# A three-block transformer stack on one core: late transposes behind the next products, and a gated-attention recurrence by 128 tokens

## The chip, the cores and the metric

The kernel runs on one core of one Trainium2 chip. The metric is the device time of one execution in microseconds (us), the median of several runs. TensorE (PE) does the matrix products, VectorE (DVE), ScalarE (ACT) and GpSimd (POOL) the elementwise work, SyncE (SP) issues most transfers. A matrix product reads its stationary operand by a weight load (PEld) of its own and writes to PSUM, which has eight banks here: two named mm, three a, three t.

## The reference

A sequence of 512 tokens of width 1024 (float32) goes through a first block with three branches side by side (gated linear attention, sparse attention over the best 128 keys, cross attention to 256 memory tokens), and then two blocks A and B, each with a mixer, an output projection and an FFN of 2816. Every sublayer has a norm before and after it:

```python
x = x + rmsnorm(merged @ w_o, g_post)          # first block
for l in range(2):
    h = rmsnorm(x, g_mix_pre[l])
    mix = concat([main(h), memory_attention(h)]) @ w_out[l]
    x = x + rmsnorm(mix, g_mix_post[l])
    x = x + rmsnorm(swiglu(rmsnorm(x, g_ffn_pre[l]), w_ffn_in[l], w_ffn_out[l]), g_ffn_post[l])
```

The gated attention (4 heads, keys of 128, values of 256) works in chunks of 64 tokens. With b the running sum of the log gates in a chunk:

```python
q_d = q * exp(b); k_d = k * exp(-b); k_t = k * exp(b_last - b); decay = exp(b_last)
o = tril(q_d @ k_d.T) @ v + q_d @ state       # per chunk and head
state = decay * state + k_t.T @ v
```

## The kernel before

**Products.** Every large product is made of float32 halves: `mm3` (lines 372 to 375) issues high x high, high x low and low x high, so one unit of a 1024-deep weight is 24 matmuls. `unit_T` (404) multiplies one weight block of 128 columns by all 512 tokens (512 columns a matmul), `units_half` (414) takes several weight blocks and does tokens 0 to 255 of all of them before tokens 256 to 511 (256 columns a matmul), `units_N` (427) gives tokens as rows. The plain float32 products of the recurrence and the transposes through the identity are not split; such a product leaves two records in the trace, a transpose one.

**Weights.** Weights come in one packed array, in the order of use. `load_more` (297) issues the transfers on SP into 47 general slots of [128, 1024] (`get`, `put`: the slot that has been free longest is taken first); some weights are scaled on GpSimd as they land (line 310). `do_piece` (334) splits them: ScalarE makes the high half (336), VectorE, or GpSimd where `ctl["lo"]` says so, the low half (337). `ctl["ahead"]` and `ctl["stage"]` say how many weights are split and loaded ahead, and a split begins only while four slots are free (`keep`).

**Order.** The kernel is one unrolled program. Side work (attention blocks) is written as generators that `pump` steps between units. The framework then orders the instructions of each engine itself: by its own estimate of when an instruction's inputs are ready, and among the ready ones by program order. So the order on an engine can differ from that of the program.

**Sublayer ends.** `close_sublayer` (1133) does an output projection for four blocks of 128 tokens. For each block: 48 products into a pair of banks, then `to_T` (492) of the block before (eight transposes through a bank of kind t, ScalarE's high half, VectorE's low half), then `residual` (1100: square sums on ScalarE, the gain product z in 1107, the reciprocal root, x in 1113) and `prenorm` (1121: square sums, reciprocal root, hn in 1128 or 1130). After the fourth block its `to_T` follows at once. `wout` (1301) calls it three times: for `wo` ahead of `mem_kv` (1175, memory keys and values of A), for `awo` and `bwo` ahead of the FFN (1238), which opens with `units_half` over g0, u0, g1, u1 and g2. The FFN's own end (1280 to 1296) has the same loop with banks t t, t a, a a, mm mm for the four blocks; after A's FFN come `mem_kv` of B and the keys `kvk0`, `kvk1` by `units_half` (1619).

**The reciprocal root** (443) is a bit-trick start and two refinements on VectorE, for one value per partition (n = 1) eight instructions: 450, 455, 462, 463, 455, 465, 466 behind the sums of 1091 and 1094.

```python
V.scalar_tensor_tensor(t, y_, v, y_, op0=OP.mult, op1=OP.mult)            # 455
V.scalar_tensor_tensor(t, t, -10.0 / 3.0, t, op0=OP.add, op1=OP.mult)     # 462
V.scalar_tensor_tensor(y, t, 5.0, g, op0=OP.add, op1=OP.mult)             # 463
```

**The recurrence.** `gq` units (954) write qd, `gk` units (971) kd and the decayed keys, which `s_kt` transposes to ktt. `s_gla` (990) is pumped between the units of `dz` and of branch d. For each block of 128 tokens: scores of all 128 x 128 pairs (1017), kept by `copy_predicated` where both tokens are in the same chunk and causal (1019); scores times values (1024); the product of the first chunk's queries with the state into rows 0 to 63 (1027); the state's update from the first chunk's 64 rows, `delta(2t)` (1003 to 1011); then the second chunk's queries with the new state into rows 64 to 127 (1033), `delta(2t + 1)`, and the head norm. The sparse attention `s_dsa` (866) reads queries dq and writes oD (913) in four slots each.

Of the kernel before, what the change touches and what calls it, by code (L numbers as in the profile page):

```python
# [20 lines left out]
D = 1024  # L21
# [137 lines left out]
def make_consts():  # L159
    cols = []  # L160
    pos = 0

    def add(name, arr):
        nonlocal pos
        a = np.zeros((128, arr.shape[1]), np.float32)
        a[:arr.shape[0]] = arr
        _C[name] = (pos, arr.shape[1])
        pos += arr.shape[1]
        cols.append(a)

# [4 lines left out]
    add("bd", ((r[:, None] <= r[None, :]) & (r[:, None] // 64 == r[None, :] // 64)).astype(np.float32))  # L175
# [29 lines left out]
def model_kernel(ctx: ExitStack, tc: tile.TileContext, A, out):  # L205
# [237 lines left out]
    def rsqrt(ss, n, scale, name):  # L443
# [8 lines left out]

        def vyy(y_):
            if n == 1:
                V.scalar_tensor_tensor(t, y_, v, y_, op0=OP.mult, op1=OP.mult)  # L455
            else:
                V.tensor_tensor(t, y_, y_, op=OP.mult)
                V.tensor_tensor(t, t, v, op=OP.mult)

# [5 lines left out]
        V.tensor_scalar(t, t, -0.5 * 0.375 ** 3, 1.5 * 0.375, op0=OP.mult, op1=OP.add)  # L465
# [26 lines left out]
    def to_T(hn, act, tt, keep=False):  # L492

        for j in range(2):
            pt = ps_t([128, 4, 128])
# [368 lines left out]
    oD = [get([128, 2, 512], F32, "oD") for _ in range(4)]  # L864

    def s_dsa():
# [51 lines left out]
        put(*wsel[0], dkT, dvh, dvl, *dq, *toep)  # L918
# [28 lines left out]

    bl = T["b"]
    qd = [get([128, 2, 512], F32, "qd") for _ in range(2)]
    kd = [get([128, 2, 512], F32, "kd") for _ in range(2)]  # L950
    ktt = [get([128, 2, 512], F32, "kt") for _ in range(2)]
    gv = [get([128, 1024], F32, "gv") for _ in range(4)]
    decay = p_c.tile([128, 4, 8], F32, name="decay")
    for h in range(4):
# [4 lines left out]
        V.scalar_tensor_tensor(qd[h // 2][:, h % 2], o, 128 ** -0.5, e, op0=OP.mult, op1=OP.mult)  # L959
        V.tensor_copy(decay[:, h], e[:, 63:512:64])  # L960
        pump()
# [9 lines left out]
    for h in range(4):  # L971
# [4 lines left out]
        V.tensor_tensor(kd[h // 2][:, h % 2], o, e, op=OP.mult)  # L976
# [4 lines left out]
        V.tensor_tensor(flat(e), o, flat(e), op=OP.mult)  # L981
# [8 lines left out]
    def s_gla():  # L990
        att = [get([128, 2, 4, 128], F32, "att")]
        POOL.memset(att[0], 0.0)
        Sb = [get([128, 4, 256], F32, "S") for _ in range(2)]
        bd = C("bd").bitcast(U32)

        def delta(c):
            t, r0 = c // 2, 64 * (c % 2)
            ds = []
            for hp in range(2):
                pa = ps_a([128, 2, 256])  # L1000
                for j in range(2):
                    h = 2 * hp + j
                    PE.matmul(pa[:, j], ktt[t // 2][r0:r0 + 64, t % 2, 128 * h:128 * h + 128],  # L1003
                              gv[t][r0:r0 + 64, 256 * h:256 * h + 256], start=True, stop=True)
                for j in range(2):
                    h = 2 * hp + j
                    if c == 0:
                        V.tensor_copy(Sb[1][:, h], pa[:, j])
                    else:
                        V.scalar_tensor_tensor(Sb[(c + 1) % 2][:, h], Sb[c % 2][:, h], decay[:, h, c:c + 1],  # L1010
                                               pa[:, j], op0=OP.mult, op1=OP.add)

        for t in range(4):
            tk = slice(128 * t, 128 * t + 128)
            pa = ps_a([128, 4, 128])
            for h in range(4):
                PE.matmul(pa[:, h], kd[h // 2][:, h % 2, tk], qd[h // 2][:, h % 2, tk], start=True, stop=True)
            am = att[0][:, t % 2]
            V.copy_predicated(am, bd[:, None, :].to_broadcast([128, 4, 128]), pa)
            yield  # L1020
            po = [ps_t([128, 2, 256]) for _ in range(2)]
            for h in range(4):
                oo = po[h // 2][:, h % 2]
                PE.matmul(oo, am[:, h], gv[t][:, 256 * h:256 * h + 256], start=(h % 2 == 0),
                          stop=False, skip_group_check=True)
                if t:
                    PE.matmul(oo[0:64], qd[h // 2][:, h % 2, 128 * t:128 * t + 64], Sb[0][:, h],
                              start=False, stop=False, skip_group_check=True)
            delta(2 * t)
            yield  # L1030
            for h in range(4):
                oo = po[h // 2][:, h % 2]
                PE.matmul(oo[64:128], qd[h // 2][:, h % 2, 128 * t + 64:128 * t + 128], Sb[1][:, h],
                          start=False, stop=True, skip_group_check=True)
            if t < 3:
                delta(2 * t + 1)
# [11 lines left out]
        put(*att, *Sb, *qd, *kd, *ktt)  # L1048
# [39 lines left out]
    def sums(s2, n):  # L1088
# [44 lines left out]
    def close_sublayer(key, act, gpost, g, a):  # L1133
# [4 lines left out]
        prev = None  # L1138
        for t in range(5):
            if t < 4:  # L1140
                cols = HALVES if t < 3 else LAST
                y = [(ps_a if t % 2 else ps_mm)() for _ in cols]
                for n, sl in enumerate(cols):
                    for k in range(8):
                        mm3(y[n][:, :sl.stop - sl.start], act.hi(k)[:, 128 * t:128 * t + 128], act.lo(k)[:, 128 * t:128 * t + 128],
                            ws[k].hi[:, 0, sl], ws[k].lo[:, 0, sl], k == 0, k == 7)
                tick(2)
                if t == 3:
                    drop(*ws)
                    act.drop()  # L1150
                    ctl["ahead"], ctl["stage"] = 2, 3
            if prev is not None:
                to_T(prev, a, t - 1)
            if t < 4:
                sx = residual(y, t, gpost, cols)
                prev = prenorm(t, sx, g)
            pump()
        ctl["lo"] = None

# [15 lines left out]
    def mem_kv(a, p):  # L1175
# [13 lines left out]
        units_N(f"{p}mv", a, 2, lambda t, o: ACT.activation(v[:, t], o, AF.Copy), ps_a)  # L1189
# [48 lines left out]
    def ffn(p, l, hT, more, side={}):  # L1238
# [4 lines left out]
        first = units_half([f"{p}g0", f"{p}u0", f"{p}g1", f"{p}u1", f"{p}g2"], hT)  # L1243
# [14 lines left out]
        banks = [[ps_t(), ps_t()], [ps_t(), ps_a()], [ps_a(), ps_a()], [ps_mm(), ps_mm()]]  # L1258
# [20 lines left out]
        prev = None  # L1279
        for t in range(5):  # L1280
            if t < 4:
                for n in range(2):
                    for k in range(NFF - NR, NFF):
                        step(k, ws[k - NFF + NR], banks[t][n], t, HALVES[n])
                tick(2)
                if t == 3:
                    drop(*ws)
                    for j in range((NFF - NR) // 2, NFF // 2):
                        act.drop_group(j)
                    ctl["ahead"], ctl["stage"] = 2, 3  # L1290
            if prev is not None:
                to_T(prev, nxt, t - 1)
            if t < 4:
                sx = residual(banks[t], t, gpost, more=more)
                if more:
                    prev = prenorm(t, sx, None)
        gpost.drop()
        ctl["lo"] = None
        return nxt

    def wout(key, act, gpost, gnext):
        gp, g, a = Gain(*gpost), Gain(*gnext), Act(8, "hT")
        close_sublayer(key, act, gp, g, a)
        gp.drop()
        g.drop()
        return a

    memA = mem_prep(0)
    hA = wout("wo", mg, ("g_post",), ("g_mix_pre_2", 0))
    kvm = mem_kv(memA, "a")  # L1310
# [168 lines left out]
    hF = wout("awo", mix, ("g_mix_post_2", 0), ("g_ffn_pre_2", 0))  # L1479
# [30 lines left out]
    hB = ffn("a", 0, hF, True, sides_a)  # L1510
    cosT, sinT = T["rot"]
    memB = T["mem"]
    kvB = mem_kv(memB, "b")
# [123 lines left out]
    hF = wout("bwo", mix, ("g_mix_post_2", 1), ("g_ffn_pre_2", 1))  # L1637
    ffn("b", 1, hF, False)
# [39 lines left out]
```

## Time and profile before

| | |
|---|---|
| median of 3 runs | 2064.12 us (2061.5 to 2064.39) |
| the profiled execution | 2061.36 us, of which the span of its instructions is 2059.6 |
| busy in the span: TensorE | 2000.4 us (97%) |
| VectorE, ScalarE, GpSimd | 1098.4, 807.3, 258.7 us |
| mean granted clock of TensorE | 0.988 |

The profile lists, for a stretch, how long each engine was busy, and for groups of instructions their count, busy time and mean. PEclk is TensorE's granted clock as a share of the full one; it has two levels, 0.50 (1.2 GHz) and 1.00 (2.4 GHz), and values between are means. A matmul's end is modelled and laps over the start of the next.

### The profile page before, as it was taken

What the parts mean: (1) busy time and instruction counts of PE and PEld (TensorE: products, weight loads), DVE (VectorE), ACT (ScalarE), POOL (GpSimd) and SP (SyncE); (2) the same over time, 40 slices, a digit from 0 to 9 for tenths busy, and PEclk for the clock granted to TensorE, in tenths of its full rate; (3) what the DMA queues carried; (4) which work ended last, traced back from release to release, by engine and by line L of the source; (5) the groups of instructions that cost most, each with busy time, mean ns of one, the idle gap of its engine ahead of it and who ended that gap; (6) DMA issues with size and microseconds to landing.
All of it is one profiled execution on the core that took longest, in us unless ns stands there. A gap on an engine that the chain in (4) does not pass through costs nothing.

```text
span 2059.6 us, 26847 instructions
## 1 busy us (share of the span) xinstructions
PE 2000.4 (97%) x10234; PEld 1679.4 (82%) x10234; DVE 1098.4 (53%) x2463; ACT 807.3 (39%) x1787; POOL 258.7 (13%) x214
## 2 busy tenths in 40 slices
PE   7999999999999999999998999999989989999998
PEld 6888878889777888898887888888787778888886
DVE  8744996354654342763677443342668873332423
ACT  5533553244423241444544342232336843322311
POOL 7201100000111111100022111102130021111000
PEclk9999999999999999999999999999999999999999
DMA  6321232122222343232124122144121232322421
GB/s 261 120 72 52 64 113 84 60 82 74 80 72 75 99 144 102 82 126 92 53 81 154 57 93 92 62 154 143 32 82 42 83 126 69 102 72 72 143 73 41
DMA packets 54528, 189.57 MB, mean 92 GB/s; under 512 B 6648, under 2 KB 8832, under 8 KB 54400
## 3 DMA queue, kind: packets, MB, share of 16 engines
q1 hardware_dynamic: 52640, 185.36, 27.5%
q0 software_dynamic: 464, 1.44, 0.3%
q8 instruction: 80, 1.31, 0.3%
q10 hardware_dynamic: 1296, 1.07, 0.2%
q14 instruction: 48, 0.39, 0.1%
HBM read 185.73 MB, written 2.11 MB: 91 GB/s over the span
## 4 chain that ended last, share of the span: by engine, by line
PE 88%; DVE 8%; ACT 2%; issue 1%; DMA 1%; SPq 0%; DVEq 0%; ACTq 0%
PE mm L373 21%; PE mm L375 21%; PE mm L374 21%; PE pa L373 4%; PE pa L375 4%; PE pa L374 4%; PE pt L374 1%; PE pt L375 1%; PE pt L373 1%; PE pt L497 1%; DVE rst L455 1%; PE pa L529 1%; PE pa L1003 1%; PE pa L880 1%; PE pt L1435 1%
## 5 line engine op out<-in xcount | busy, mean ns | idle before, releaser
L509 POOL TENSOR_TENSOR ffal<-t,ffah 128x512 fp32r<-128x512 f32 x44 | 61.3, 1393 | 420.8 <-ACT ffah L508 420.8
L1251 DVE SCALAR_TENSOR_TENSOR t<-t,mm 128x512 f32<-128x512 f32 x42 | 28.8, 685 | 82.5 <-PE mm L375 82.5
L374 PE MATMUL mm<-hTl,h_au 128*128 128x512 f32 (+1 forms) x176 | 66.9, 380 | 0.0
L373 PE MATMUL mm<-hTh,h_bu 128*128 128x512 f32 (+1 forms) x176 | 66.9, 380 | 0.0
L375 PE MATMUL mm<-hTh,l_au 128*128 128x512 f32 (+1 forms) x176 | 66.9, 380 | 0.0
L374 PE MATMUL mm<-hTl,h_bu 128*128 128x512 f32 (+1 forms) x176 | 66.9, 380 | 0.0
L373 PE MATMUL mm<-hTh,h_au 128*128 128x512 f32 (+1 forms) x176 | 66.9, 380 | 0.0
L375 PE MATMUL mm<-hTh,l_bu 128*128 128x512 f32 (+1 forms) x176 | 66.9, 380 | 0.0
L497 PE MATMUL pt<-ident,hn 128*128 128x128 f32 x192 | 31.6, 303 | 34.6 <-DVE hn L1130 19.4
L373 PE MATMUL mm<-hTh,h_ag 128*128 128x512 f32 (+1 forms) x168 | 63.9, 380 | 0.0
L374 PE MATMUL mm<-hTl,h_ag 128*128 128x512 f32 (+1 forms) x168 | 63.8, 380 | 0.0
L375 PE MATMUL mm<-hTh,l_ag 128*128 128x512 f32 (+1 forms) x168 | 63.8, 380 | 0.0
L373 PE MATMUL mm<-hTh,h_bg 128*128 128x512 f32 (+1 forms) x168 | 63.8, 380 | 0.0
L375 PE MATMUL mm<-hTh,l_bg 128*128 128x512 f32 (+1 forms) x168 | 63.7, 379 | 0.0
L374 PE MATMUL mm<-hTl,h_bg 128*128 128x512 f32 (+1 forms) x168 | 63.7, 379 | 0.0
L1248 ACT ACTIVATE t<-mm 128x512 f32<-128x512 f32 x40 | 23.7, 592 | 95.6 <-PE mm L375 95.6
L1249 DVE SCALAR_TENSOR_TENSOR t<-t,mm 128x512 f32<-128x512 f32 x40 | 27.4, 684 | 57.7 <-ACT t L1248 57.7
L497 PEld LDWEIGHTS pt<-ident,hn 128*128 128x128 f32 x192 | 23.9, 154 | 40.1 <-issue 28.1
L508 ACT ACTIVATE ffah<-t 128x512 fp32r<-128x512 f32 x44 | 27.5, 624 | 74.2 <-DVE t L1251 74.1
L337 DVE TENSOR_TENSOR l_ay<-w_ay,h_ay 128x512 fp32r<-128x512 f32 x44 | 29.3, 713 | 45.7 <-ACT h_ay L336 33.9
L337 DVE TENSOR_TENSOR l_bu<-w_bu,h_bu 128x512 fp32r<-128x512 f32 x38 | 25.6, 691 | 49.0 <-PE mm L374 21.3
L337 DVE TENSOR_TENSOR l_by<-w_by,h_by 128x512 fp32r<-128x512 f32 x44 | 29.1, 712 | 37.1 <-ACT h_by L336 23.1
(947 smaller groups left out, 6583.2 us busy)
## 6 DMA issues: line engine op xcount, KB each, us to landing
w_ag<-in_wpk SPq DMA_DIRECT2D x22, 512.0 KB, 4.0
w_au<-in_wpk SPq DMA_DIRECT2D x22, 512.0 KB, 4.0
w_ay<-in_wpk SPq DMA_DIRECT2D x22, 512.0 KB, 3.7
w_bu<-in_wpk SPq DMA_DIRECT2D x22, 512.0 KB, 3.6
w_bg<-in_wpk SPq DMA_DIRECT2D x22, 512.0 KB, 3.6
w_by<-in_wpk SPq DMA_DIRECT2D x22, 512.0 KB, 3.7
x<-in_x SPq DMA_DIRECT2D x8, 512.0 KB, 6.4
w_mk<-in_wpk SPq DMA_DIRECT2D x8, 512.0 KB, 6.1
```

The source lines that it names most:

```text
L337: (ctl["lo"] or V).tensor_tensor(l, s, f(h), op=OP.subtract)
L373: PE.matmul(o, lh, rh, start=first, stop=False)
L374: PE.matmul(o, lh, rl, start=False, stop=False)
L375: PE.matmul(o, ll, rh, start=False, stop=last)
L455: V.scalar_tensor_tensor(t, y_, v, y_, op0=OP.mult, op1=OP.mult)
L497: PE.transpose(pt[:, k], hn[:, 512 * j + 128 * k:512 * j + 128 * k + 128], ident)
L508: ACT.activation(h, src, AF.Copy)
L509: POOL.tensor_tensor(l, src, f(h), op=OP.subtract)
L529: PE.matmul(o, st[:, j, tk], kh, start=True, stop=False)
L1248: ACT.activation(t, og, AF.Tanh, scale=0.5)
L1249: V.scalar_tensor_tensor(t, t, 1.0, og, op0=OP.add, op1=OP.mult)
L1251: V.scalar_tensor_tensor(t, t, 0.5, ou, op0=OP.mult, op1=OP.mult)
```

## The change

1. *Late transposes.* `close_sublayer` no longer transposes the last token block; it returns a function that does. `mem_kv` calls it after the first half of the memory values, `units_half` in the FFN before the first token half of its fifth unit. At the end of A's FFN the banks are handed out in another order, blocks 0 and 1 are transposed after blocks 1 and 2 through banks just read, and blocks 2 and 3 in the deferred function. `kvk0` and `kvk1` become two `unit_T`.
2. *Reciprocal root.* For n = 1 every step, and the sum's second step, is a `tensor_scalar` whose other operands are pointer scalars.
3. *Recurrence.* Queries and keys are kept per head as three groups of 64 tokens, [first chunk, joining copy, second chunk]: the queries' copy is the second chunk times the first one's decay, the keys' copy the first chunk decayed to its end. A block of 128 tokens then has one state update and one state product of full height and width; the scores of each query chunk are one product with 128 key rows.
4. *Slots.* oD is dq: the sparse attention's outputs overwrite its queries.

```diff
+        if n == 1:
+            t, t1, w, w1 = [sm(1, f"rs{c}") for c in "abcd"]
+            V.tensor_scalar(t, g, v, g, op0=OP.mult, op1=OP.mult)
+            V.tensor_scalar(t1, t, -10.0 / 3.0, t, op0=OP.add, op1=OP.mult)
+            V.tensor_scalar(y, t1, 5.0, g, op0=OP.add, op1=OP.mult)
+            V.tensor_scalar(w, y, v, y, op0=OP.mult, op1=OP.mult)
+            V.tensor_scalar(w1, w, a, b, op0=OP.mult, op1=OP.add)
+            r = sm(1, "rsr")
+            V.tensor_scalar(r, y, w1, None, op0=OP.mult)
+            return r
...
-            V.scalar_tensor_tensor(v, s2[:, i:i + 1], 1.0 / D, u, op0=OP.mult, op1=OP.add)
+            V.tensor_scalar(v, s2[:, i:i + 1], 1.0 / D, u, op0=OP.mult, op1=OP.add)
...
-    def units_half(keys, act):
+    def units_half(keys, act, late):
...
             for c, o in zip(cs, os_):
+                if t == 0 and c is cs[-1]:
+                    late()
...
-    oD = [get([128, 2, 512], F32, "oD") for _ in range(4)]
+    oD = dq
...
+        for i, w in ((0, 0), (1, 2)):
+            V.scalar_tensor_tensor(dst[:, :, w], halves(o)[:, :, i], 128 ** -0.5, halves(e)[:, :, i],
+                                   op0=OP.mult, op1=OP.mult)
         V.tensor_copy(decay[:, h], e[:, 63:512:64])
+        V.tensor_tensor(dst[:, :, 1], dst[:, :, 2], decay[:, h, 0::2, None].to_broadcast([128, 4, 64]), op=OP.mult)
+        V.tensor_tensor(decay2[:, h], decay[:, h, 0::2], decay[:, h, 1::2], op=OP.mult)
...
+        V.tensor_tensor(kk[h][:, :, 1], halves(o)[:, :, 0], e4[:, :, 0], op=OP.mult)
+        V.tensor_tensor(e4[:, :, 1], halves(o)[:, :, 1], e4[:, :, 1], op=OP.mult)
+        V.tensor_tensor(e4[:, :, 0], kk[h][:, :, 1], decay[:, h, 1::2, None].to_broadcast([128, 4, 64]), op=OP.mult)
...
+        for t in range(4):
+            pa = ps_a([128, 4, 128])
+            for h in range(4):
+                for i in range(2):
+                    PE.matmul(pa[:, h, 64 * i:64 * i + 64], flat(kk[h][:, t, i:i + 2]), qq[h][:, t, 2 * i],
+                              start=True, stop=True)
...
+            for hp in range(2 if t < 3 else 0):
                 pa = ps_a([128, 2, 256])
                 for j in range(2):
                     h = 2 * hp + j
+                    PE.matmul(pa[:, j], ktt[t // 2][:, t % 2, 128 * h:128 * h + 128],
+                              gv[t][:, 256 * h:256 * h + 256], start=True, stop=True)
...
+                    PE.matmul(oo, flat(qq[h][:, t, 0:2]), Sb[t % 2][:, h], start=False, stop=True,
+                              skip_group_check=True)
...
+            if t:
+                to_T(hn, a, t - 1)
+            sx = residual(y, t, gpost, cols)
+            hn = prenorm(t, sx, g)
             pump()
...
+        return lambda: to_T(hn, a, 3)
...
+        def keep_v(t, o):
+            ACT.activation(v[:, t], o, AF.Copy)
+            if t == 0:
+                late()
...
-        banks = [[ps_t(), ps_t()], [ps_t(), ps_a()], [ps_a(), ps_a()], [ps_mm(), ps_mm()]]
+        pools = [[ps_mm, ps_mm], [ps_a, ps_a], [ps_a, ps_t], [ps_t, ps_t]]
+        banks = [[f_() for f_ in fs] for fs in pools]
...
+            if more and t in (1, 2):
+                to_T(rows[t - 1], nxt, t - 1, bank=pools[t - 1])
...
+        def rest():
+            for t in (2, 3):
+                to_T(rows[t], nxt, t, bank=pools[t])
...
-    o0, o1 = units_half(["kvk0", "kvk1"], hB)
-    ACT.activation(kr[:, 0], o0, AF.Copy)
-    ACT.activation(kr[:, 1], o1, AF.Copy)
     for i in range(2):
+        o = unit_T(f"kvk{i}", hB)
+        ACT.activation(kr[:, i], o, AF.Copy)
         start(s_ropek(i))
```

## Rows read from the trace of the kernel before

**Rows 1.** Busy time by stretch: TensorE, weight loads, VectorE, ScalarE, GpSimd, clock, DMA

```profile
0.00:80.00 80.00, 63.08 (x443) 60.30 (x444) 71.92 (x138) 46.52 (x94) 47.92 (x44) 0.94 0.61 220
460.00:535.00 75.00, 74.86 (x492) 64.44 (x491) 38.44 (x87) 37.22 (x88) 0.00 (x0) 1.00 0.24 78
535.00:640.00 105.00, 105.00 (x450) 76.19 (x450) 58.55 (x128) 37.02 (x87) 14.16 (x11) 1.00 0.21 66
...
1100.00:1130.00 30.00, 21.07 (x156) 20.89 (x156) 24.20 (x44) 16.22 (x38) 14.98 (x12) 0.83 0.57 209
...
1480.00:1520.00 40.00, 31.66 (x217) 30.29 (x216) 36.27 (x73) 19.51 (x45) 18.96 (x16) 0.87 0.33 106
...
1676.00:1702.00 26.00, 17.09 (x127) 16.92 (x126) 21.81 (x40) 15.61 (x36) 14.97 (x12) 0.80 0.62 225
```

**Rows 2.** Waits of TensorE: total us, times, longest us

```profile
PE pt L497 <- DVE hn L1130: 19.4, 3, 8.9
PE pt L497 <- DVE hn L1128: 8.0, 3, 5.5
```

**Rows 3.** TensorE's timeline at awo's end: start, us, [idle before, releaser]

```profile
1104.33 0.37 PE L373 MATMUL mm<-hTh,h_ag 128*128 128x256 f32 x1
...
1120.93 1.09 PE L497 MATMUL pt<-ident,hn 128*128 128x128 f32 x4 [8.93 <-DVE hn L1130]
```

**Rows 4.** Busy time and clock after that wait, columns as in rows 1

```profile
1120.00:1122.00 2.00, 1.07 (x5) 1.10 (x6) 1.97 (x4) 0.00 (x0) 0.00 (x0) 0.50 0.05 18
...
1126.00:1128.00 2.00, 2.00 (x16) 2.00 (x15) 2.00 (x5) 1.37 (x3) 0.00 (x0) 0.80 0.39 84
```

**Rows 5.** Groups of VectorE, 1104 to 1121: busy us, mean ns, idle before

```profile
L463 DVE SCALAR_TENSOR_TENSOR rsy<-rst,rsi 128x1 f32<-128x1 f32 x2 | 2.2, 1100 | 0.0
L455 DVE SCALAR_TENSOR_TENSOR rst<-rsy,ssv 128x1 f32<-128x1 f32 x2 | 2.2, 1090 | 0.0
L462 DVE SCALAR_TENSOR_TENSOR rst<-rst 128x1 f32<-128x1 f32 x2 | 1.9, 938 | 0.0
...
L455 DVE SCALAR_TENSOR_TENSOR rst<-rsi,ssv 128x1 f32<-128x1 f32 x2 | 1.2, 622 | 0.1
L466 DVE TENSOR_TENSOR rsy<-rsy,rst 128x1 f32<-128x1 f32 x2 | 1.2, 596 | 0.1
...
L450 DVE TENSOR_SCALAR rsi<-ssv 128x1 int32<-128x1 int32 x2 | 0.3, 154 | 0.1
```

**Rows 6.** Timelines of VectorE and of GpSimd

```profile
1120.03 1.42 DVE L1130 SCALAR_TENSOR_TENSOR hn<-x,rsy,gain 128x512 f32<-128x512 f32 x2
...
1457.72 0.16 DVE L463 SCALAR_TENSOR_TENSOR rsy<-rst,rsi 128x1 f32<-128x1 f32 x1
...
1106.97 2.56 POOL L337 TENSOR_TENSOR l_au<-w_au,h_au 128x512 fp32r<-128x512 f32 x2
...
1055.34 0.99 DVE L450 TENSOR_SCALAR rsi<-rsv 128x4 int32<-128x4 int32 x1
```

**Rows 7.** TensorE's timeline in the recurrence (two records are one product)

```profile
539.66 1.99 PE L1024 MATMUL pt<-gv,att 128*128 128x256 f32 x8
...
548.33 1.94 PE L1033 MATMUL pt<-S,qd 128*64 128x256 f32 x8
...
557.70 1.05 PE L1017 MATMUL pa<-qd,kd 128*128 128x128 f32 x8
...
564.04 0.59 PE L1024 MATMUL pt<-gv,att 128*128 128x256 f32 x2
...
568.76 1.99 PE L1003 MATMUL pa<-gv,kt 64*128 64x256 f32 x8
```

**Rows 8.** The first 75 us: one wait of TensorE, one group of VectorE

```profile
PE pt L497 <- DVE hn L489: 5.2, 4, 3.3
...
L455 DVE SCALAR_TENSOR_TENSOR rst<-rsi,rsv 128x1 f32<-128x1 f32 x6 | 3.9, 643 | 0.1
```

**Rows 9.** DMA issues by tile: engine, count, size, median us to landing

```profile
w_ag<-in_wpk SPq DMA_DIRECT2D x22, 512.0 KB, 4.0
```

More of the change, by code (lines that the diff above doesn't have):

```diff
@@ L948, in model_kernel @@
     bl = T["b"]
[L949 to L950 removed]
+    qq = [get([128, 4, 3, 64], F32, "qq") for _ in range(4)]
+    kk = [get([128, 4, 3, 64], F32, "kk") for _ in range(4)]
     ktt = [get([128, 2, 512], F32, "kt") for _ in range(2)]
@@ L975, in model_kernel @@
         ACT.activation(e, b, AF.Exp, scale=-1.0 / 16.0)
-        V.tensor_tensor(kd[h // 2][:, h % 2], o, e, op=OP.mult)
+        for i, w in ((0, 0), (1, 2)):
+            V.tensor_tensor(kk[h][:, :, w], halves(o)[:, :, i], halves(e)[:, :, i], op=OP.mult)
         e = t2([128, 8, 64])
@@ L1024, in s_gla @@
                 PE.matmul(oo, am[:, h], gv[t][:, 256 * h:256 * h + 256], start=(h % 2 == 0),
-                          stop=False, skip_group_check=True)
+                          stop=(t == 0), skip_group_check=True)
                 if t:
-                    PE.matmul(oo[0:64], qd[h // 2][:, h % 2, 128 * t:128 * t + 64], Sb[0][:, h],
-                              start=False, stop=False, skip_group_check=True)
-            delta(2 * t)
+                    PE.matmul(oo, flat(qq[h][:, t, 0:2]), Sb[t % 2][:, h], start=False, stop=True,
+                              skip_group_check=True)
             yield
[L1031 to L1036, printed above, removed]
             put(gv[t])
@@ L1137, in close_sublayer @@
         ctl["ahead"], ctl["lo"] = 1, POOL
[L1138 to L1156, printed above, removed]
+        for t in range(4):
+            cols = HALVES if t < 3 else LAST
+            y = [(ps_a if t % 2 else ps_mm)() for _ in cols]
+            for n, sl in enumerate(cols):
+                for k in range(8):
+                    mm3(y[n][:, :sl.stop - sl.start], act.hi(k)[:, 128 * t:128 * t + 128], act.lo(k)[:, 128 * t:128 * t + 128],
+                        ws[k].hi[:, 0, sl], ws[k].lo[:, 0, sl], k == 0, k == 7)
+            tick(2)
+            if t == 3:
+                drop(*ws)
+                act.drop()
+                ctl["ahead"], ctl["stage"] = 2, 3
+            if t:
+                to_T(hn, a, t - 1)
+            sx = residual(y, t, gpost, cols)
+            hn = prenorm(t, sx, g)
             pump()
+        gpost.drop()
+        g.drop()
         ctl["lo"] = None
+        return lambda: to_T(hn, a, 3)
     def mem_prep(l):
@@ L1236, in mem_block, with ffn @@
             put(*qs, *kv)
-    def ffn(p, l, hT, more, side={}):
+    def ffn(p, l, hT, late, more, side={}):
         gpost = Gain("g_ffn_post_2", l)
@@ L1242, in ffn @@
         ctl["lo"] = POOL
-        first = units_half([f"{p}g0", f"{p}u0", f"{p}g1", f"{p}u1", f"{p}g2"], hT)
+        first = units_half([f"{p}g0", f"{p}u0", f"{p}g1", f"{p}u1", f"{p}g2"], hT, late)
         ctl["lo"] = None
@@ L1278, in ffn @@
         nxt = Act(8, "hT") if more else None
[L1279 to L1296, printed above, removed]
+        rows = []
+        for t in range(4):
+            for n in range(2):
+                for k in range(NFF - NR, NFF):
+                    step(k, ws[k - NFF + NR], banks[t][n], t, HALVES[n])
+            tick(2)
+            if t == 3:
+                drop(*ws)
+                for j in range((NFF - NR) // 2, NFF // 2):
+                    act.drop_group(j)
+                ctl["ahead"], ctl["stage"] = 2, 3
+            if more and t in (1, 2):
+                to_T(rows[t - 1], nxt, t - 1, bank=pools[t - 1])
+            sx = residual(banks[t], t, gpost, more=more)
+            if more:
+                rows.append(prenorm(t, sx, None))
         gpost.drop()
         ctl["lo"] = None
-        return nxt
+        def rest():
+            for t in (2, 3):
+                to_T(rows[t], nxt, t, bank=pools[t])
+        return nxt, rest
     def wout(key, act, gpost, gnext):
[L1302 to L1306, printed above, removed]
+        a = Act(8, "hT")
+        return a, close_sublayer(key, act, Gain(*gpost), Gain(*gnext), a)
     memA = mem_prep(0)
-    hA = wout("wo", mg, ("g_post",), ("g_mix_pre_2", 0))
-    kvm = mem_kv(memA, "a")
+    hA, late = wout("wo", mg, ("g_post",), ("g_mix_pre_2", 0))
+    kvm = mem_kv(memA, "a", late)
     aux = get([128, 896], F32, "aux")
```

67 lines of the change are left out of this document (28 added, 39 removed).

## The prediction

> **What bounds the kernel now.** I read the table by stages first [rows 1]. From 535 to 640 us, where the gated attention's recurrence is interleaved with weight products, TensorE is busy 105.00 us of 105.00 and VectorE 58.55: only less matmul time helps there. In four other stretches TensorE rests: 16.9 us of the first 80, 8.9 from 1100 to 1130, 8.3 from 1480 to 1520, 8.9 from 1676 to 1702; the granted clock's mean is lower there too (0.94, 0.83, 0.87, 0.80). The waits come next [rows 2]: 19.4 us in three waits of the transposes (line 497) for hn of line 1130, the longest 8.9, and 8.0 in three for hn of line 1128. Those are the ends of the sublayers.
>
> One end close up, the out-projection of block A. Program order puts the last transposes ahead of the FFN's first units, but TensorE first ran 62 matmuls of those, from 1104.33 to 1112.0, and then waited 8.93 us [rows 3]. So the framework places the transposes where its own estimate has hn ready, and hn was 9 us later than that. After the wait TensorE ran at 0.50, the lower of its two levels (1.2 GHz), until about 1126.8 [rows 4].
>
> Why hn is late is seen on VectorE [rows 5]: ten one-element steps of the two reciprocal roots (lines 455, 462, 463, 466) took 8.7 us, 0.6 to 1.1 each, while one-element tensor_scalars beside them (line 450) took 0.154. In a quiet stretch the same line 463 takes 0.16 [rows 6]. GpSimd was subtracting weight halves back to back then, 2.56 us for two. So a step that reads two SBUF tensors waits for the GpSimd instruction in front of it, and a one-element tensor_scalar doesn't. A four-element tensor_scalar of line 450 took 0.99 us elsewhere, so more elements can wait [rows 6].
>
> **1. Recurrence by 128 tokens.** Four half-height delta products take 1.99 us, four half-width ones 1.94, four full-array ones 1.99, four score products 1.05 [rows 7]. Each row laps about 0.1 over the next, so 1.9, 1.9, 1.9 and 0.9. Where full and half-width products alternate, eight take 4.72 (568.76 - 564.04), 0.9 more than two groups of four. Blocks 1 and 2 now cost 0.9 + 4.7 + 3 x 1.9 = 11.3 each, block 3 one delta less, 9.4, block 0 0.9 + 4 x 1.9 = 8.5: 40.5 in all. After: three groups of deltas, four of score-times-value, three of state products, all full-array: 10 x 1.9 = 19.0. The score products become 32 of 64 columns instead of 16 of 128. No row has 64 columns: if the time goes with the columns they still cost 4 x 0.9 = 3.6, if with the instructions 7.2; I take the middle, 5.4, as columns and weight loads both count. Together 24.4, a gain of 16.1 (14.3 to 17.9), all on the path. Alternation disappears with it.
>
> The Trainium skill, TensorEngine Tiling (Array Packing), Key Properties, speaks against this part: tiles of a half-used array work independently, so half-size products could overlap. Rows 7 do not agree: four half-height products cost what four full ones do. By that rule the fourteen half-size groups would have cost some 13 us less than they did, and this part would gain 3.
>
> VectorE gets more to do ahead of it: for each of eight units some two more instructions of 256 columns. Two of 512 take 1.42 [rows 6], so about 0.4 each and under 1 us per unit; 16 state updates fall away later. From 460 to 535 us it is busy 38.4 of 75 [rows 1]; TensorE's own units hide it, and if that cover were gone, 8 us would show.
>
> **2. The one-element steps as tensor_scalars.** With two pointer scalars no row shows this form. Bounds: 0.154 as line 450 under the same GpSimd load, or 1.1 as line 463 [rows 5]. It reads one tensor of one element, as line 450 does, so I take 0.2. The ten steps then take 2 instead of 8.7, and hn starts near 1113 instead of 1120.0 [rows 6]. Its two halves and the x update read two tensors each and still wait; first half ready near 1114.
>
> **3. The late transposes.** After the two out-projections that feed an FFN they stand behind four half units, 4 x 24 matmuls of 0.124 us (7.67 / 62): from 1104.3 to 1116.2, past 1114. The wait of 8.9 goes, and so does the low clock after it, 5.9 us at half rate, 2.9: 11.8. The end at 1676 to 1702 has the same wait to 0.02 and the same pattern: 11.8 again. Behind the transposes stand only the fifth half unit and then the second halves, which need these tokens; their copies by ScalarE and VectorE have that unit's 3 us. The queues of SP and GpSimd are not moved past: transposes issue no transfer. hn's slot is held some 10 us longer.
>
> After the first out-projection they go behind 72 matmuls of the memory keys and values; the third wait of line 1130 is what 19.4 leaves, 1.6: gain 1 (0 to 1.6).
>
> At the first FFN's end two blocks are deferred, and key units no longer start on half their tokens. Before: 5.5 us of wait for block 3 and the other 2.5 of the 8.0 mostly for block 2 [rows 2], and a clock mean of 0.87 over 40 us, about 5 us [rows 1]: 13. After: block 2's wait goes, but all that can run before block 3 is memory keys and values, 96 matmuls, 11.9 us; the 11 key matmuls that ran ahead now come after, and the first key unit waits for block 3's copies. VectorE is busy 36.3 of these 40 us, GpSimd 19, so hn 3 gains perhaps 4 us. I take a gain of 2; bounds a gain of 9 (both waits shrink, clock kept) and a loss of 6 (block 3 as late as now: 3 more of wait, 3 for the copies).
>
> **4. Prologue.** TensorE waits 5.2 us for hn of line 489 there, and line 455 takes 0.64 us on the mean [rows 8]. The same replacement shortens six roots where GpSimd is busy 47.9 of 80 us. Gain 4 (0 to 9, the waits and part of the low clock).
>
> **5. At nothing:** the output tiles of the sparse attention written over its queries (each query block is read before; four slots freed, and four more taken by the recurrence), the FFN's bank order (matmuls into the pair that is still being read can go after the others; with that cover gone, one evacuation at each of two FFNs), the tail's chain (as in the quiet stretch a step is 0.16 already).
>
> **Sum.** 16.1 + 11.8 + 11.8 + 1 + 2 + 4 = 46.7. The profiled run took 2061.4 (span 2059.6 and 1.8 around it): 2014.7. The median shown, 2064.1, is 2.7 above it, so on that footing 2017. With all terms at their good ends 17.9 + 23.6 + 1.6 + 9 + 9 = 61 is gained, 2003; at their poor ends, with the chain shortened, 14.3 + 23.6 - 6 = 32, 2032.
>
> **Rivals.**
> Pointer scalars wait as well: the chain keeps its length, the transposes come at 1120.9, and TensorE reaches them at 1116.2: 4.7 of wait remain with the low clock behind it, a gain of 4.2 per end; prologue and FFN end give nothing. 16.1 + 8.4 + 1 = 25.5 and 2064.1 - 25.5 = 2038.6. For it: the four-element tensor_scalar's 0.99 [rows 6]. Against: one-element ones did not, 0.154 [rows 5]. Chance 0.11. The Trainium skill, SBUF - State Buffer, "SBUF: two separate sides", has an exclusive lock between GpSimd and a VectorE instruction with two SBUF inputs or in a two-port mode; if the new form took a two-port mode, the result would be this one.
>
> The order doesn't change: the framework again puts the transposes at its estimate, 1112. With the chain shorter 2 to 3 us of wait remain per end: 19 for two ends instead of 23.6, 2022. Chance 0.09.
>
> Slower: the slots. During the 24 units from the second gate on, the recurrence holds eight query and key tiles instead of four, and the old queries live on as outputs. By my count 9 or 10 of 47 slots stay free; three staged weights and one split pair take 5, and a split begins only while 4 are free. If a count is one or two off, the prefetch stops and each unit shows the landing of its weight, 4.0 us [rows 9]: 24 x 4.0 = 96, less 46.7, gives 2113. It decides from 2.1 us per unit. Against: in the present kernel the stage from 535 has no wait. Chance 0.03.
>
> Terms cancelling to within 4 us, which is 0.2% and about what a measurement of this kernel can tell from no change: 0.02. My forecast: 0.75, own range 2003 to 2032. The whole range, 2002 to 2038, reaches from its good end over the unchanged order to just short of the pointer-scalar case. Faster 0.95, same 0.02, slower 0.03.
>
> **What would show it.** Lines 455 to 466 with one element at about 0.2 us in 1100 to 1120; no wait above 1 us at the two FFN starts and a clock of 1.00 through them; recurrence products in 24 to 25 us and 32 score products; a wait of 5 to 8 us still there at the first FFN's end. Wrong would make it: one-element tensor_scalars near 1 us, transposes ahead of the fourth half unit, or weight waits in the gate units.

## The result and the profile after

The changed kernel takes 2025.14 us (median of 4 runs, 2022.6 to 2028.04) where the kernel before takes 2062.81 beside it: a ratio of 0.9819, 95% interval 0.9801 to 0.9838. That is faster by 37.7 us, a little under 2%; 46.7 were forecast. The profiled execution took 2024.41, its span 2022.6, 37.0 less than before.

The table of stages first, of the changed kernel (columns as in rows 1; the stretches lie earlier by what has been gained until then):

```profile
0.00:80.00 80.00, 68.19 (x465) 64.03 (x466) 72.24 (x144) 47.52 (x97) 52.60 (x45) 0.96 0.62 225
455.00:530.00 75.00, 74.86 (x496) 64.37 (x494) 38.63 (x87) 37.20 (x87) 0.00 (x0) 1.00 0.22 71
530.00:618.00 88.00, 88.00 (x420) 74.54 (x418) 53.13 (x113) 37.46 (x89) 14.54 (x11) 1.00 0.28 90
1080.00:1106.00 26.00, 23.79 (x184) 23.18 (x183) 21.34 (x43) 16.60 (x38) 17.62 (x12) 0.93 0.68 254
1450.00:1490.00 40.00, 32.31 (x194) 28.21 (x193) 38.38 (x82) 21.81 (x50) 20.20 (x15) 0.91 0.33 106
1646.00:1672.00 26.00, 23.79 (x184) 23.18 (x183) 21.37 (x41) 16.83 (x37) 16.08 (x12) 0.93 0.67 250
```

The recurrence's stretch is still full of TensorE and VectorE has room in it. At the two FFN starts TensorE now rests 2.2 us of 26, where it rested 8.9 [rows 1]; at the first FFN's end it still rests 7.7 of 40. The waits of TensorE (total, times, longest) name what is left:

```profile
PE pt L509 <- DVE hn L1147: 4.9, 1, 4.9
PE mm L372 <- DVE mv L525: 3.9, 3, 3.0
PE pt L509 <- DVE hn L1149: 3.8, 4, 1.0
PE pa L373 <- DVE l_amv.1_7657 L336: 2.3, 1, 2.3
...
PE pa L372 <- ACT mkv L1210: 1.8, 1, 1.8
...
PE mm L372 <- DVE t L1276: 1.5, 2, 1.3
PE mm L373 <- DVE l_gv0.0_4095 L336: 1.0, 1, 1.0
```

Line 1149 is the old 1130, 1147 the old 1128 [rows 2]: 19.4 us of waits at the three out-projections have become 3.8, in four waits of up to 1.0. New are the waits for the low half of the memory-value weights (l_amv.1) at the first out-projection's end, for the copied memory values (mkv) at the first FFN's end, and for the last reader of an FFN bank (line 1276). The wait for mv in the prologue has grown to 3.9 from 0.8. The last line, in the gate units, comes back with the first experiment.

Where the 37.0 us came from is read from the starts of TensorE's first product with given weights, in each kernel's own trace; a stage is the time between two such starts, in us. The last four columns are experiments, told further below.

| stage (from, to) | forecast gain | before | after | gain | recurrence back | roots back | places back | banks back |
|---|---|---|---|---|---|---|---|---|
| prologue (0, iq) | 4 | 83.96 | 79.06 | 4.9 | 77.31 | 85.57 | 80.64 | 77.62 |
| gates (iq, dz) | 0 | 428.92 | 428.97 | -0.05 | 427.04 | 429.01 | 428.97 | 428.97 |
| recurrence (dz, gz) | 16.1 | 186.77 | 169.18 | 17.6 | 186.70 | 169.22 | 169.19 | 169.19 |
| first out-projection's end (amk, aqk) | 1 | 49.22 | 50.29 | -1.1 | 49.26 | 52.27 | 51.20 | 50.46 |
| A's FFN start (ag, ay) | 11.8 | 255.79 | 248.42 | 7.4 | 248.41 | 251.17 | 250.98 | 248.41 |
| A's FFN products (ay, bmk) | 0 | 122.01 | 122.64 | -0.6 | 122.71 | 122.62 | 122.65 | 122.19 |
| first FFN's end (bmk, bmq) | 2 | 51.41 | 47.36 | 4.1 | 48.15 | 51.22 | 49.51 | 47.39 |
| B's FFN start (bg, by) | 11.8 | 253.23 | 246.34 | 6.9 | 246.32 | 249.09 | 248.16 | 246.33 |
| B's FFN products and end (by, end) | 0 | 127.57 | 129.46 | -1.9 | 128.98 | 128.92 | 129.49 | 127.89 |

Three stages vary from run to run with the same instructions: over the kernels whose products there are those of the changed kernel, the prologue took 77.3 to 81.0, the first out-projection's end 49.3 to 50.5, the first FFN's end 46.7 to 49.4. In these a difference within that spread (3.7, 1.2 and 2.7 us), in one profile, shows nothing. The recurrence repeats to 0.1 in every kernel. The FFN starts repeat to 0.2 in most, but A's is 1.4 longer in one later kernel, and 1.1 shorter in another, where nothing was edited; the gates are 1.1 longer in two.

The FFN start of block A close up, TensorE's timeline and the clock behind it (columns as in rows 3 and rows 4):

```profile
1094.67 0.28 PE L374 MATMUL pa<-hTh,l_au 128*128 128x256 f32 x1
1095.82 0.63 PE L509 MATMUL pt<-ident,hn 128*128 128x128 f32 x4 [0.87 <-DVE hn L1149]
1097.50 0.63 PE L509 MATMUL pt<-ident,hn 128*128 128x128 f32 x4 [1.05 <-DVE hn L1149]
```

```profile
1098.00:1100.00 2.00, 2.00 (x13) 2.00 (x12) 2.00 (x3) 0.38 (x1) 0.49 (x1) 0.58 0.75 205
1100.00:1102.00 2.00, 2.00 (x13) 2.00 (x12) 2.00 (x5) 0.96 (x2) 0.00 (x0) 0.57 1.03 307
```

The transposes stand where the code puts them, behind the fourth half unit, and still wait twice, 1.9 us in all. Behind the second wait, from 1098 on, the clock was at its lower level for most of 4 us, which takes another 1.7 (4 x 0.43). VectorE shows why hn was late:

```profile
1086.00 0.27 DVE L463 TENSOR_SCALAR rsc<-rsy,ssv 128x1 f32<-128x1 f32 x1
1086.31 0.15 DVE L464 TENSOR_SCALAR rsd<-rsc 128x1 f32<-128x1 f32 x1
1086.49 0.21 DVE L466 TENSOR_SCALAR rsr<-rsy,rsd 128x1 f32<-128x1 f32 x1
1086.74 3.02 DVE L1132 SCALAR_TENSOR_TENSOR x<-z,rsr,x 128x512 f32<-128x512 f32 x2
...
1092.36 0.21 DVE L466 TENSOR_SCALAR rsr<-rsy,rsd 128x1 f32<-128x1 f32 x1
1092.49 1.49 DVE L336 TENSOR_TENSOR l_au<-w_au,h_au 128x512 fp32r<-128x512 f32 x1
1093.90 3.45 DVE L1149 SCALAR_TENSOR_TENSOR hn<-x,rsr,gain 128x512 f32<-128x512 f32 x2
```

The one-element steps are at 0.15 to 0.27 us, and the root is done at 1092.5. But a weight piece of 1.49 us (l_au) now stands between the root and hn, and hn's two halves take 3.45 where they took 1.42 [rows 6].

The recurrence in TensorE's timeline (two records are one product):

```profile
549.06 1.89 PE L1029 MATMUL pa<-qq,kk 128*128 128x64 f32 x16
556.34 1.89 PE L1038 MATMUL pa<-gv,kt 128*128 128x256 f32 x8
558.06 0.59 PE L1050 MATMUL pt<-gv,att 128*128 128x256 f32 x2
558.49 0.59 PE L1053 MATMUL pt<-S,qq 128*128 128x256 f32 x2
```

Eight score products of 64 columns take as long as four products of 256; from one start to the next a group is 1.72 (558.06 - 556.34). Score-times-value and state products alternate at 0.43 a product, with no extra time.

### The profile page after: what moved, and what is told of

It is laid out like the page before. It is cut to its first block, busy times and chain, and to the rows that moved or that the text cites. A ratio compares the mean times of both kernels' runs of the same rounds, so it can differ in the third digit from the quotient of the medians.

```text
span 2022.6 us, 26679 instructions
## 1 busy us (share of the span) xinstructions
PE 1980.6 (98%) x10154; PEld 1670.1 (83%) x10154; DVE 1098.3 (54%) x2471; ACT 807.3 (40%) x1787; POOL 270.9 (13%) x214
## 4 chain that ended last, share of the span: by engine, by line
PE 83%; DVE 11%; ACT 2%; DMA 2%; issue 2%; POOL 0%; SPq 0%; DVEq 0%; ACTq 0%
PE mm L373 20%; PE mm L372 20%; PE mm L374 20%; PE pa L373 4%; PE pa L372 4%; PE pa L374 4%; PE pt L374 1%; PE pt L373 1%; PE pt L372 1%; DVE w L774 1%; DVE m L773 1%; PE pa L892 1%; DVE x L1132 1%; PE pt L1461 1%; PE pt L509 1%
## 5 line engine op out<-in xcount | busy, mean ns | idle before, releaser
L1126 DVE TENSOR_TENSOR z<-mm,gain 128x512 f32<-128x512 f32 x16 | 11.0, 689 | 73.2 <-ACT t L1125 73.2
L951 POOL TENSOR_TENSOR merged<-merged,t 128x512 f32<-128x512 f32 x16 | 25.1, 1571 | 156.2 <-DVE t L949 156.2
```

The costliest lines, as they stand in the source:

```text
L951: POOL.tensor_tensor(m, m, t, op=OP.add)
```

## The experiments

**Each part undone alone.** Four kernels, each the changed one with one part as before.

```diff
# recurrence back: the old chunks of 64 tokens (oD stays on dq)
# roots back
-            V.tensor_scalar(t, g, v, g, op0=OP.mult, op1=OP.mult)
+                V.scalar_tensor_tensor(t, y_, v, y_, op0=OP.mult, op1=OP.mult)
...
# places back, at each of the four ends
+    late_()
+    late = lambda: None
# banks back
-        pools = [[ps_mm, ps_mm], [ps_a, ps_a], [ps_a, ps_t], [ps_t, ps_t]]
+        pools = [[ps_t, ps_t], [ps_t, ps_a], [ps_a, ps_a], [ps_mm, ps_mm]]
...
-                to_T(rows[t - 1], nxt, t - 1, bank=pools[t - 1])
+                to_T(rows[t - 1], nxt, t - 1)
...
-                to_T(rows[t], nxt, t, bank=pools[t])
+                to_T(rows[t], nxt, t)
```

> Only the recurrence goes back to 64 tokens. Theory (the changed trace's own shift across that stage): 17.6 us come back, 2043. By the terms of the forecast 16.1, 2041. Rival (half-size products overlap, so full-array ones save little): 3, 2028. The stages after the recurrence keep their lengths to 0.3 us.

Measured: 2038.28 us, ratio to before 0.9889 (0.9874 to 0.9904). The recurrence's own stage is 17.5 longer (186.70), as the theory said, so the rival of overlapping half-size products falls for products as they stand here: the four of a group all lie on the same half of the array (lines 1003 and 1027 of the kernel before). Products on different halves, one behind the other, were not run. In all the kernel lost 13.1, not 17.5: 1.9 came back in the gate stage (427.04), and the rest lies in the three stages that vary. This edit also takes VectorE's added work out of the gate units. The changed kernel waits 1.0 us there for l_gv0.0, a weight's low half that VectorE makes; this kernel doesn't, and the kernel before waits 0.5. So the added work may cost TensorE about a microsecond. The rest of the 1.9 is open: the kernel before, with the same gate code, does not show it (428.92).

> Only the one-element steps go back to their old forms. Theory: prologue +4.9; at each FFN start the first half of hn comes 5.0 us after the transposes' place instead of 0.9, so +3 to +4 each; first FFN's end +0 to +4; first out-projection -1.1 (its loss belongs to the longer quiet steps). Sum 13, 2038 (2033 to 2043). Rival A (the FFN starts are won by the place of the transposes alone): only the prologue's 4.9 comes back, 2030. Rival B (won by the short steps alone): 4.9 + 14 + 4, 2048.

Measured: 2039.25, ratio 0.9892 (0.9878 to 0.9907); 14.1 lost. The FFN starts lose 2.75 each, the first FFN's end 3.9, the prologue 6.5. The transposes of the FFN start in A wait once:

```profile
PE pt L501 <- DVE hn L1141: 4.9, 1, 4.9
```

That is the expected 5.0. What the steps run beside matters too:

```profile
1099.33 2.41 DVE L1124 SCALAR_TENSOR_TENSOR x<-z,rsy,x 128x512 f32<-128x512 f32 x2
...
1105.70 1.19 DVE L460 SCALAR_TENSOR_TENSOR rst<-rsy,ssv 128x1 f32<-128x1 f32 x1
...
1107.31 1.41 DVE L1141 SCALAR_TENSOR_TENSOR hn<-x,rsy,gain 128x512 f32<-128x512 f32 x2
```

GpSimd makes low halves of weights back to back until 1106.9 here and until 1098.5 in the changed kernel. With the slow steps hn comes after that burst and is quick (1.41); with the short steps it falls inside it and takes 3.45. So part of what the steps give is taken back by hn and by x. The first out-projection's end did not shorten as expected; it was 2.0 longer.

> Only the late transposes go back to directly behind their rows, where the framework places them by its own estimate. Theory: at the FFN starts they then stand behind three half units, 24 matmuls (2.9 us) earlier, so the wait is 2.9 longer: +3 to +4 each; at the first FFN's end 41 matmuls earlier, +3 to +5; first out-projection 0. Sum 10, 2035. Rival (the place is worth nothing, short steps did it all): 2025.

Measured: 2031.49, ratio 0.985 (0.9834 to 0.9866); 6.4 lost. The FFN starts lose 2.6 and 1.8; the first FFN's end loses 2.2, which is within that stage's spread. So the places count at the FFN starts, by somewhat less than expected, and the rival falls. From before, short steps without new places give 4.8 at A's FFN start, new places without short steps 4.6, both together 7.4: they overlap, since either alone shortens the same wait.

> Only the FFN's order of accumulator banks goes back. Theory: the wait of 1.33 us for the last gate product's reader goes from the second FFN and the 0.6 lost at the first: -1.6 and -0.6, 2023; nothing else moves. Rival (the loss has another cause): no change, 2025.

Measured: 2022.65, ratio 0.9812 (0.9797 to 0.9827), a median 2.5 below the changed kernel's. Its products stages are 122.19 and 127.89, 0.5 and 1.6 shorter, and no wait for line 1276 is left in either. B's products take 127.6 to 128.0 in every kernel with the old order and 128.9 to 129.5 in every one with the new. The bank order is a loss, as the theory said; the kernels that follow have the old order.

**What keeps hn late.** Each of these four is the last kernel (old banks) with one edit; the fourth has the first one's edit too.

```diff
# late transposes split, in units_half: in the middle of the last half unit and behind it
+                for k in range(8):
+                    if t == 0 and c is cs[-1] and k == 4:
+                        late((0,))
...
+                    late((1,))
...
# GpSimd idle at the FFN starts
-        ctl["lo"] = POOL
         first = units_half(...)
# GpSimd at the first out-projection's end
+    ctl["lo"] = POOL
     kvm = mem_kv(memA, "a", late)
...
+    ctl["lo"] = None
# key units by halves (on top of the split)
-    for i in range(2):
-        o = unit_T(f"kvk{i}", hB)
+    for i, o in enumerate(units_half(["kvk0", "kvk1"], hB, late[1])):
...
```

> On top of u4: at both FFN starts the first four late transposes go into the middle of the fifth half unit (12 matmuls, 1.44 us, later), the last four behind it (2.9 us later). Theory (the transposes' place is still too early for hn: 0.87 and 1.05 us of wait and the low clock behind them): both waits and the low clock go, the copies hide behind the 12 matmuls: -3 to -4 per end, 7 in all, 2015.5. Rival (the copies of the late tokens become the wait, about 1 us at 0.5 to 1.0 clock): -1 per end, 2020.5.

Measured: 2030.46 (one run). The transposes wait no more, but A's FFN start is 251.11 instead of 248.41 and B's 248.49 instead of 246.33. One wait took the place of the two, and VectorE's timeline shows what stands ahead of the copies:

```profile
PE mm L373 <- DVE hTl L517: 4.2, 1, 4.2
```

```profile
1098.53 1.77 DVE L336 TENSOR_TENSOR l_au<-w_au,h_au 128x512 fp32r<-128x512 f32 x1
1100.23 1.28 DVE L336 TENSOR_TENSOR l_ag<-w_ag,h_ag 128x512 fp32r<-128x512 f32 x2
1101.43 1.28 DVE L336 TENSOR_TENSOR l_au<-w_au,h_au 128x512 fp32r<-128x512 f32 x2
1102.63 1.28 DVE L336 TENSOR_TENSOR l_ag<-w_ag,h_ag 128x512 fp32r<-128x512 f32 x2
1103.84 0.41 DVE L517 TENSOR_TENSOR hTl<-pt,hTh 128x256 fp32r<-128x256 f32 x1
```

Seven weight pieces for later units, 5.3 us, are ahead of the first copy of the late tokens. Both theories missed this: the wait is neither gone nor 1 us, but VectorE's queue.

> On top of u4: at the FFN starts VectorE instead of GpSimd makes the low halves of the weights. Theory (GpSimd's port stretches the x update and hn): two x updates take 1.4 us instead of 3.0 and two hn 1.4 instead of 3.5 there. Rival (VectorE's own queue): both stay stretched. On the time: VectorE gets 12 x 0.68 = 8 us more in a stretch of 22 of which it was busy 18.7, so hn comes no earlier and the time is the same or up to 8 us longer, 2023 to 2031.

Measured: 2021.28 (one run). The two rows that the theories differ on:

```profile
1091.72 1.40 DVE L1132 SCALAR_TENSOR_TENSOR x<-z,rsr,x 128x512 f32<-128x512 f32 x2
...
1099.74 1.41 DVE L1149 SCALAR_TENSOR_TENSOR hn<-x,rsr,gain 128x512 f32<-128x512 f32 x2
```

With GpSimd idle, x and hn take 1.40 and 1.41, so it is GpSimd that stretches them to 3.0 and 3.5. The Trainium skill, SBUF - State Buffer, "Who interferes with whom", has VectorE with two SBUF inputs contend with GpSimd's reads; this agrees. VectorE's extra pieces stand between the steps instead, hn comes later, and the framework moved the transposes behind the fifth half unit, where they wait 2.0. The two FFN starts are 0.6 and 0.3 shorter, too little to count in one profile.

> On top of u4: from the first out-projection's end to the value and gate units GpSimd makes the low halves of the weights instead of VectorE. Theory (VectorE's queue is what delays l_amv.1 there: 4.1 us of wait and 1.5 of low clock): the stage from the first memory-key product to the first query product shrinks by 3 to 5 us, 2019. Rival (GpSimd's port stretches the chain there as it does at the FFN starts): the same or longer, 2023 or more.

Measured: 2030.33 (one run); the first out-projection's end is 55.70 instead of 50.46. The rival's time came: a single wait for hn of 7.0 us took the place of the wait for l_amv.1. Its reason is only part of it. x takes 3.07 beside GpSimd there (1.42 without), but hn starts no later behind the stage's first product (16.4 us, against 16.6 in the kernel with old banks). What is new is the order: the framework put the transposes behind 36 products of the memory values, where 62 products, some of them of the next weights, had stood ahead of them. (A's FFN start, where nothing was edited, was 1.4 longer in this profile; that is not explained.)

> On top of v1: at the first FFN's end the fourth block's transposes go into the fifth... the second key unit's first half, both key units being run by token halves: up to 4.3 us of matmuls more in front of hn. Theory (hn is late): the wait of 4.9 and its low clock of 2 mostly go, -4 to -6 against v1. Rival (VectorE's queue: the key weights' low halves are ready no earlier than hn): TensorE waits for l_kvk instead, 0 to -1 against v1.

Measured: 2031.16 (one run). The first FFN's end is 50.59, against 49.40 in the kernel with the split alone: no gain. The wait for hn is gone (0.2) and three others stand in its place:

```profile
PE mm L374 <- DVE l_kvk L336: 4.0, 2, 2.3
PE mm L373 <- DVE hTl L517: 3.3, 1, 3.3
PE mm L372 <- ACT hTh L516: 2.6, 1, 2.6
```

**Clearing VectorE around hn.** The pieces ahead of hn and of its copies belong, by the order of use, to the FFN's third input unit and its fourth and fifth pairs of units. In the next two kernels GpSimd makes them (with old banks; the second has the split places too).

```diff
         first = units_half(...)
-        ctl["lo"] = None
         for i in range(NFF):
+            if i == 5:
+                ctl["lo"] = None
```

> On top of u4: GpSimd keeps making the low halves of the weights until the fifth gate unit of each FFN, so no such piece stands on VectorE between the last reciprocal root, hn and the copies of the late tokens. Theory (the one piece of 1.5 us ahead of hn is what made it late): hn's first half is there 0.5 us before its transposes' place instead of 0.9 behind it; the first wait goes, the second is about 0.6; with the low clock -2 to -3.5 per end, 2017.5 (2015.5 to 2019). Rival (GpSimd's port keeps hn late, and its longer queue delays the second gate units' weights): 0 or a loss, 2022 or more.

Measured: 2017.35, ratio 0.9783 (0.9768 to 0.9797). The FFN starts are 245.39 and 243.36, 3.0 shorter each, with one wait of 0.4 for hn left in each:

```profile
PE pt L509 <- DVE hn L1149: 0.4, 1, 0.4
```

> v1 and v5 together: the late transposes in the middle of the fifth half unit and behind it, and no weight piece on VectorE around hn and its copies. Theory (in v1 the seven pieces ahead of the copies made the wait of 4.2 us): no wait over 0.5 us at the two FFN starts and a clock of 1.00; -3.5 per end against u4, 2015.5. Rival (the copies themselves are slow under GpSimd's load): a wait of 1 to 2 us for hTl remains, 2019.

Measured: 2014.71, ratio 0.9771 (0.9754 to 0.9787). The FFN starts are 244.60 and 242.48, 3.8 shorter each, no wait, and the clock at full speed; the whole of A's (columns as in rows 1), and hn:

```profile
1083.00:1106.00 23.00, 22.90 (x190) 22.50 (x189) 14.21 (x32) 14.22 (x33) 23.00 (x18) 1.00 0.65 234
```

```profile
1092.28 0.21 DVE L468 TENSOR_SCALAR rsr<-rsy,rsd 128x1 f32<-128x1 f32 x1
1092.53 3.07 DVE L1151 SCALAR_TENSOR_TENSOR hn<-x,rsr,gain 128x512 f32<-128x512 f32 x2
```

hn follows the root at once. It is still stretched (3.07), since GpSimd is busy 23.00 of 23, but nothing waits for it. So the split that lost 4.9 at the two starts by itself (2.7 and 2.2) gains 1.7 (0.8 and 0.9) once VectorE's queue is clear; the two kernels that follow repeat both lengths to 0.3.

**The first FFN's end.** There 7 us of wait were left. Two more kernels on top of the last:

```diff
# memory-key copies on ScalarE (both lines)
-                V.tensor_copy(kh[64 - 64 * j:128 - 64 * j, 2 * u + j], f(kh[s, 2 * u + j]))
+                ACT.activation(kh[64 - 64 * j:128 - 64 * j, 2 * u + j], f(kh[s, 2 * u + j]), AF.Copy)
# and the gains of B's query weights on ScalarE, in load_more
+                    if key.startswith("b"):
+                        for r in range(n * q, n * q + n):
+                            ACT.activation(w3[:, r], w3[:, r], AF.Copy, scale=small[:, g0 + m + r:g0 + m + r + 1])
+                        continue
```

> On top of v6: the sixteen copies of the memory keys to the other half of the partitions go from VectorE to ScalarE. Theory (VectorE's queue makes hn late at the first FFN's end: eight copies of 0.29 us lie among the last block's root steps and updates): hn comes 2.0 to 2.4 us earlier, the wait of 6.9 us falls to about 4.7, with the clock -2 to -3; first out-projection's end 0 to -1.5; 2011.5 in all (2010 to 2013). Rival (hn's time there is set by GpSimd's gains and ScalarE): no change, 2014.7.

Measured: 2013.85, ratio 0.9771 (0.9758 to 0.9784): no change. The wait for hn did fall, to 1.3 at the longest, more than the theory said. But the stage is 49.09 (48.65 without the edit): the waits moved on to the value weights and the token copies, and the clock stayed low. The first out-projection's end, with the same copies moved, did not shorten either (51.01, against 49.44 without the edit).

> On top of v7: ScalarE instead of GpSimd multiplies the gains into the second block's query weights, so GpSimd rests at the first FFN's end. Theory (GpSimd's port stretches the last two blocks' hn and x there: 2.5, 3.0 and 2.0 us instead of 0.9, 1.4 and 0.9): hn some 2 to 3 us earlier, -2 to -4 against v7. Rival (ScalarE's 64 more instructions of about 0.25 us delay the copies of tokens and the splits): the same or up to 5 longer.

Measured: 2008.97, ratio 0.9745 (0.9732 to 0.9759). The first FFN's end is 41.80, 7.3 shorter. VectorE's rows for the last two blocks:

```profile
1452.75 0.88 DVE L1153 TENSOR_SCALAR hn<-x,rsr 128x512 f32<-128x512 f32 x2
1458.44 1.40 DVE L1138 SCALAR_TENSOR_TENSOR x<-z,rsr,x 128x512 f32<-128x512 f32 x2
1465.66 0.87 DVE L1153 TENSOR_SCALAR hn<-x,rsr 128x512 f32<-128x512 f32 x2
```

In the changed kernel the same three are 2.52, 2.98 and 1.99. The stretch from 1450 to 1490 in the kernels before these two edits, with the first, and with both, one fence each:

```profile
1450.00:1490.00 40.00, 32.16 (x190) 27.82 (x190) 36.17 (x71) 19.23 (x44) 20.13 (x16) 0.87 0.27 94
```

```profile
1450.00:1490.00 40.00, 34.80 (x190) 29.54 (x188) 31.44 (x64) 22.99 (x53) 19.37 (x16) 0.83 0.32 101
```

```profile
1450.00:1490.00 40.00, 37.95 (x247) 34.19 (x247) 30.10 (x70) 38.31 (x103) 2.65 (x2) 0.96 0.27 93
```

TensorE's busy time grew with the first edit too, but at a clock of 0.83, so the number of its products in the stretch stayed (190). Only with GpSimd idle as well did it do 247 there; the gains moved without the copies were not run. This last kernel beats the changed one and the one before.

## Why the prediction was right, and which terms were mis-sized

The direction, the parts and their order of size held, and the time, 2025.1, lies 8.1 above the 2017.0 forecast, inside the range. It is nearer than its terms were: the recurrence, the prologue and the first FFN's end gave 4.5 more than forecast, the FFN starts, the first out-projection's end and the bank order 13.9 less. That part of the errors cancelled is luck.

*Term 1, the recurrence*: 16.1 forecast, 17.6 measured, the products as counted. The 64-column scores took 4 x 1.72 = 6.9, near the upper bound (the time goes with the instructions); the ten full groups took 1.72 each instead of 1.9. VectorE's extra work ahead of it was put at nothing; against before nothing shows (428.97 to 428.92), but the kernel without it is 1.9 shorter there, of which a wait of 1.0 is VectorE's. The prediction also read rows 7 as speaking against overlap on separate halves of the array; those groups use one half each, so they do not test it.

*Term 2, the short steps*: right in size, 0.15 to 0.27 instead of 0.6 to 1.2; the ten take 2.3 (2 x (0.27 + 0.21 + 0.21 + 0.27 + 0.21)), 2 were forecast. The rival of waiting pointer scalars falls.

*Term 3, the FFN starts*, is the one that failed: 11.8 each were forecast, 7.4 and 6.9 came. The cover was as counted: transposes due 11.8 us behind the first gate product (1094.95 - 1083.20; forecast 11.9). The failed step is "first half ready near 1114", 9.7 us behind that product; it was ready at 12.6 (1095.82 - 1083.20). Of these 2.9 us, 0.7 is the root's end (1092.57 instead of 8.7 behind that product), 1.3 the weight piece that the framework put between root and hn, and 0.9 the half itself, 1.9 until the transposes began instead of 1.0. I had said that hn would still wait for GpSimd and had not priced both halves: the second came 1.7 later and made a second wait. Together they cost 1.9 of wait and 1.7 of low clock; of the other 0.8, 0.3 is a wait for the token copies and 0.5 is not placed. The kernel that clears the queue shows the rest: 255.79 - 244.60 = 11.2 and 253.23 - 242.48 = 10.8, close to 11.8.

*The first out-projection's end*: forecast +1, measured -1.1, within what that stage varies by; no experiment settles its sign. What one profile shows is a piece of l_amv.1 that VectorE got to only after x, with the wait of 2.3.

*The first FFN's end*: forecast +2 with bounds of -6 and 9, measured 4.1. The roots carry it (3.9 when put back); what the places give (2.2) is not clear of the stage's spread. I had VectorE's load there as the limit. Relieving VectorE alone changed nothing (49.09 against 48.65), and taking GpSimd's gains away on top of that gave 7.3.

*Term 4, the prologue*: forecast 4, measured 4.9; over all kernels with the short steps there its mean is 79.5, against 83.96 and 85.57 with the old. The waits for hn, rst and rsv there fell from 9.1 to 1.0, and 3.1 of that went to the wait for mv.

*Term 5, at nothing*: the bank order was not free. The prediction named the price, one evacuation at each FFN, and took the products into other banks for its cover; the 1.3 us wait shows that the cover wasn't there, and the products stages lost 0.6 and 1.9 (0.5 and 1.6 came back with the old order). The slots did hold: no wait for a weight's landing appears in the gate units.

The unchanged order, a rival at 2022, came nearest in time, but for another reason: the order did change, and hn was late.

## What to carry to other kernels

Work moved ahead of a wait is worth only what the late producer still lacks: price every instruction between the producer's input and its consumer's copies, those that the framework hoists in between included. When a chain gets shorter, look at what it now runs beside; here hn slid into GpSimd's burst and gave back two of some six microseconds. And an engine with much idle time (ScalarE is busy 40% of the span) may be the place for work that stretches a neighbour, even where it takes more instructions.

## What the runs showed of the hardware that was not expected

A one-element tensor_scalar with one pointer operand took 0.21 us and with two 0.27, beside a busy GpSimd as in quiet, while the old two-tensor forms take 0.16 and 0.22 in quiet and up to 1.2 beside it. A 512-wide tensor_scalar with one tensor input does not share this; it is stretched: two halves of hn took 0.88 with GpSimd idle and 2.52 beside it. The Trainium skill, SBUF - State Buffer, "Who interferes with whom", lists tensor_scalar among the operations that can contend; the wide rows agree, the one-element rows show that it does not reach them.

A plain float32 product of 128 rows by 64 columns cost as much as one by 128: eight in 1.72 us here, four in 0.9 before, 0.22 each.

Two waits of 0.87 and 1.05 us with 0.6 us of transposes between them were followed by a granted clock of 0.58 and 0.57 for 4 us; after the single wait of 8.9 the lower level lasted 5.9 [rows 4].
